# A row-variance kernel: sixteen-column loads in two buffers, a re-cut tail, the columns' last results stored apart, and the wait for the store moved behind the context's end

## The chip, the cores and the metric

The kernel runs on one core of one Trainium2 chip. The metric is the device time in microseconds of one execution. The kernel before takes 165.64 us (median of three runs, 165.6 to 165.7).

## What is computed

For each of 32 x 512 = 16,384 rows of 1,024 float32 values, the mean of the squares less the square of the mean, which is the row's variance:

```python
def setup_inputs():
    batch, seq, dim = 32, 512, 1024
    return {"x": np.random.randn(batch, seq, dim).astype(np.float32)}

def reference(x):
    mean_sq = np.mean(x**2, axis=-1)
    sq_mean = np.mean(x, axis=-1)**2
    return (mean_sq - sq_mean).astype(np.float32)
```

The input is 67.1 MB, the output 64 KB.

## The kernel before

The 16,384 rows are laid over 128 partitions, 128 rows to each partition. One row per partition, 128 rows in all, is called a *column*: a tile of 128 x 1024 float32, 512 KB. There are 128 columns. They form two blocks of memory (`BLOCKS`): the first 16 columns, and the other 112; within a block a partition's rows lie next to each other, so a load of n columns reads one run of n x 4 KB for each partition.

All loads are issued by SP, in order, through `load` (line 82), into one queue. The first 96 columns go in 12 loads of 8 (`GROUP`) into three buffers `xt` in turn (`NBUF`). A buffer is filled again only when `done` says that its former group is finished (line 127). The last 32 columns are the tail: loads of 8, 6, 6, 4, 3, 2 and 1 columns (`END_LOADS`), then the last two columns in two halves each. The first of these goes to `xt[0]`, the others to `xt_end`, which nothing else uses, so SP issues all of them in a row after a single wait (line 129).

Two engines work on each group. DVE (VectorE) computes a column's statistics with two `bn_stats` of 512 elements (line 100) and joins them with one `bn_aggr` (line 163), which gives mean and variance. ACT (ScalarE) needs two passes over a column: a copy scaled by -S/D that sums up to the negative mean (line 104), and a square with that mean as bias that sums up to the variance (line 109). In each group of 8, ACT has the first three columns (`NACT`), DVE the other five. DVE takes the group's arrival (`landed`), lets ACT go, and its last `bn_aggr` waits for ACT's `act_done` before it signals `done`. Both engines run this part as a loop of four turns (`Fori`) of three groups. GpSimd copies the variances of a turn from `stage` to `mv` (line 146).

In the tail, `END_WHO` gives one letter for each column: A for ACT, D for DVE. DVE's order there: first half of a column, the aggregate of the column before, second half (lines 175 to 183). The last two columns are D, each of their halves with a wait of its own (lines 186 to 199). ACT takes its columns load by load: all means, then all variances (lines 217 to 232).

SP, after the loads, stores the results of the first block (16 columns, once `copied` is up), waits for the last steps of ACT and DVE, and stores the other 112 columns. Then it clears the semaphores and waits for both stores to land (lines 235 to 242). All of this stands in one critical section (line 123). When it has ended, the tile context closes (its code has line 268 in the profile): every engine drains, they meet, and GpSimd clears the context's semaphores.

`head_slot` places the head of each loop at instruction 128 of a block of the instruction stream.

Of the kernel before, what the change touches and what calls it, by code (L numbers as in the profile page):

```python
# [7 lines left out]


# [1 line left out]
def kernel(  # L11
# [10 lines left out]

    nc = tc.nc
    P = nc.NUM_PARTITIONS
    FP32 = mybir.dt.float32
    ACTF = mybir.ActivationFunctionType
    ENG = mybir.EngineType

    xf = x.flatten_outer_dims()
    N, D = xf.shape
    assert N % P == 0
    ncols = N // P
    H = D // 2
    S = D ** -0.5

    SMALL = 16
    BLOCKS = [(0, SMALL, 0), (SMALL, ncols - SMALL, SMALL * P)]

    GROUP = 8
    NBUF = 3
    TURNS = 4
    PER_TURN = NBUF * GROUP
    END0 = TURNS * PER_TURN
    NACT = 3
    END_LOADS = [8, 6, 6, 4, 3, 2, 1]
    END_WHO = "AAADDDDD" "AADDDD" "AADDDD" "DADD" "DAD" "AD" "A"
    IN_HALVES = 2
    HEAD = 128  # L50

    pool = ctx.enter_context(tc.tile_pool(name="pool", bufs=1))
    xt = [pool.tile([P, GROUP, D], FP32, name=f"xt{b}") for b in range(NBUF)]
    xt_end = pool.tile([P, ncols - END0 - GROUP, D], FP32, name="xt_end")
    mv = pool.tile([P, 2, ncols], FP32, name="mv")
    stage = pool.tile([P, PER_TURN, 2], FP32, name="stage")
    stats = pool.tile([P, PER_TURN, 2, 6], FP32, name="stats")
    stats_end = pool.tile([P, ncols - END0, 2, 6], FP32, name="stats_end")
    neg_mean = pool.tile([P, PER_TURN], FP32, name="neg_mean")
    neg_mean_end = pool.tile([P, ncols - END0], FP32, name="neg_mean_end")  # L60
    psum = ctx.enter_context(tc.tile_pool(name="psum", bufs=1, space=bass.MemoryType.PSUM))
    junk = [pool.tile([P, D], mybir.dt.bfloat16, name=f"junk{i}") for i in range(NACT)]
    junk_sq = [psum.tile([P, D], FP32, name=f"junk_sq{i}") for i in range(NACT)]

    sync, act, dve, gps = nc.sync, nc.scalar, nc.vector, nc.gpsimd
    landed = [nc.alloc_semaphore(f"landed{b}") for b in range(NBUF)]
    NEND = len(END_LOADS) + 2 * IN_HALVES
    landed_end = [nc.alloc_semaphore(f"landed_end{b}") for b in range(NEND)]
    go = nc.alloc_semaphore("go")
    act_done = nc.alloc_semaphore("act_done")  # L70
    done = nc.alloc_semaphore("done")
    copied = nc.alloc_semaphore("copied")
    dve_step = nc.alloc_semaphore("dve_step")
    act_step = nc.alloc_semaphore("act_step")
    stored = nc.alloc_semaphore("stored")
    sems = [*landed, *landed_end, go, act_done, done, copied, dve_step, act_step]

    def load(dst, c0, n, sem, f0=0, f=D):
        b0, pitch, row0 = next(b for b in BLOCKS if b[0] <= c0 < b[0] + b[1])
# [4 lines left out]
            in_=dataclasses.replace(xf, offset=(row0 + c0 - b0) * D + f0, ap=ap),  # L84
        ).then_inc(sem, 16)

    def store(block):
        b0, pitch, row0 = block
        sync.dma_start(
            out=dataclasses.replace(out, offset=row0, ap=[[pitch, P], [1, pitch]]),  # L90
            in_=mv[:, 1, b0 : b0 + pitch],
        ).then_inc(stored, 16)

    def take(engine, sem, n):
        engine.wait_ge(sem, n)
        engine.sem_inc(sem, -n)  # L96
# [6 lines left out]
    def act_mean(i, xcol, nm):  # L103
        return act.activation(  # L104
            out=junk[i], in_=xcol, func=ACTF.Copy, scale=-S / D, accum_out=nm
        )

    def act_var(i, xcol, nm, var):
        return act.activation(  # L109
            out=junk_sq[i], in_=xcol, func=ACTF.Square, scale=S, bias=nm, accum_out=var  # L110
        )

    end_cols = []
    at = END0
    for b, n in enumerate(END_LOADS):
        for k in range(n):
            c = at + k
            col = xt[0][:, k, :] if b == 0 else xt_end[:, c - END0 - GROUP, :]
            end_cols.append((b, c, col))
        at += n  # L120
    assert at == ncols - IN_HALVES

    with tc.tile_critical(no_gpsimd_drain=True):  # L123

        for g in range(TURNS * NBUF):
            if g >= NBUF:
                sync.wait_ge(done, g - NBUF + 1)
            load(xt[g % NBUF], g * GROUP, GROUP, landed[g % NBUF])
        sync.wait_ge(done, TURNS * NBUF - NBUF + 1)
        load(xt[0], END0, GROUP, landed_end[0])  # L130
        c = END0 + GROUP
        for b, n in enumerate(END_LOADS[1:], 1):
            k = c - END0 - GROUP
            load(xt_end[:, k : k + n, :] if n > 1 else xt_end[:, k, :], c, n, landed_end[b])
            c += n
        b = len(END_LOADS)
        for c in range(c, ncols):
            for h in range(2):
                dst = xt_end[:, c - END0 - GROUP, h * H : (h + 1) * H]
                load(dst, c, 1, landed_end[b], h * H, H)  # L140
                b += 1

        gps.sem_inc(copied, 1)
        for t in range(TURNS):
# [2 lines left out]
                out=mv[:, 1, t * PER_TURN : (t + 1) * PER_TURN], in_=stage[:, :, 1]  # L147
            ).then_inc(copied, 1)

        with nc.Fori(0, TURNS, engines=[ENG.DVE], head_slot={ENG.DVE: HEAD}):  # L150
            take(dve, copied, 1)
            for b in range(NBUF):
                take(dve, landed[b], 16)
                dve.sem_inc(go, 1)
                mine = range(b * GROUP + NACT, (b + 1) * GROUP)
                for j in mine:
                    last = halves(stats[:, j, :, :], xt[b][:, j - b * GROUP, :])
                last.then_inc(dve_step, 1)
                take(dve, dve_step, 1)
                for j in mine:  # L160
                    if j == mine[-1]:
                        take(dve, act_done, 1)
                    last = dve.bn_aggr(out=stage[:, j, :], in_=stats[:, j, :, :])  # L163
                last.then_inc(done, 1)
        n = 0
        waiting = None
        seen = -1
        for b, c, col in end_cols:
            if END_WHO[c - END0] != "D":
                continue  # L170
            if b != seen:
                dve.wait_ge(landed_end[b], 16)
                seen = b
            st = stats_end[:, c - END0, :, :]
            dve.bn_stats(out=st[:, 0, :], in_=col[:, :H])  # L175
            if waiting:
                waiting()
            n += 1
            dve.bn_stats(out=st[:, 1, :], in_=col[:, H:]).then_inc(dve_step, 1)  # L179

            def waiting(n=n, c=c, st=st):
                dve.wait_ge(dve_step, n)
                dve.bn_aggr(out=mv[:, :, c], in_=st)  # L183

        b = len(END_LOADS)
        for c in range(ncols - IN_HALVES, ncols):
            st = stats_end[:, c - END0, :, :]
            col = xt_end[:, c - END0 - GROUP, :]
            dve.wait_ge(landed_end[b], 16)
            dve.bn_stats(out=st[:, 0, :], in_=col[:, :H])  # L190
            waiting()
            dve.wait_ge(landed_end[b + 1], 16)
            n += 1
            dve.bn_stats(out=st[:, 1, :], in_=col[:, H:]).then_inc(dve_step, 1)  # L194
            b += 2

            def waiting(n=n, c=c, st=st):
                dve.wait_ge(dve_step, n)
                return dve.bn_aggr(out=mv[:, :, c], in_=st)  # L199

        waiting().then_inc(dve_step, 1)
        dve_steps = n + 1

        act.preload_act_table(ACTF.Square)  # L204
        with nc.Fori(0, TURNS, engines=[ENG.Activation], head_slot={ENG.Activation: HEAD}):
            for b in range(NBUF):
                take(act, go, 1)
                mine = range(b * GROUP, b * GROUP + NACT)
                for i, j in enumerate(mine):
                    last = act_mean(i, xt[b][:, i, :], neg_mean[:, j : j + 1])  # L210
                last.then_inc(act_step, 1)
                take(act, act_step, 1)
                for i, j in enumerate(mine):
                    last = act_var(i, xt[b][:, i, :], neg_mean[:, j : j + 1], stage[:, j, 1:2])
                last.then_inc(act_done, 1)
        n = 0
        for b in range(len(END_LOADS)):
            mine = [(c, col) for bb, c, col in end_cols if bb == b and END_WHO[c - END0] == "A"]
            if not mine:
                continue  # L220
            act.wait_ge(landed_end[b], 16)
            for i, (c, col) in enumerate(mine):
                k = c - END0
                last = act_mean(i, col, neg_mean_end[:, k : k + 1])
            n += 1
            last.then_inc(act_step, 1)
            act.wait_ge(act_step, n)
            for i, (c, col) in enumerate(mine):
                k = c - END0
                last = act_var(i, col, neg_mean_end[:, k : k + 1], mv[:, 1, c : c + 1])  # L230
            n += 1
            last.then_inc(act_step, 1)
        act_steps = n

        sync.wait_ge(copied, 1)
        store(BLOCKS[0])
        sync.wait_ge(act_step, act_steps)
        sync.wait_ge(dve_step, dve_steps)
        store(BLOCKS[1])
        sync.sem_clear(range(sems[0].num, sems[-1].num + 1))  # L240
        sync.wait_ge(stored, 32)
        sync.sem_clear(stored)


# [28 lines left out]
```

## Time and profile before

| | us |
|---|---|
| median of three runs | 165.64 |
| the profiled execution | 165.63 |
| its span, first to last instruction | 163.7 |
| DVE busy | 107.0 (65%) |
| ACT busy | 107.3 (66%) |
| GpSimd busy | 1.0 (1%) |
| moved by DMA | 67.19 MB, mean 411 GB/s |
| one `bn_stats` of 512 elements in the loop | 0.679 (they overlap: ten take 6.03) |
| one aggregate in the loop | 0.177 (they overlap: four take 0.42) |
| ACT's mean, variance of a column | 1.045, 1.104 |

How to read it: the span runs from the first to the last instruction; the time of an execution also holds what lies around it. DVE's and ACT's durations are those of single instructions, and neighbouring ones overlap, so that sums are made from the starts of rows. In the row of slices each digit is the busy share of a fortieth of the span, in tenths. The chain of waits is followed back from the last instruction: at each step to what released it. A name with a q (SPq, DVEq) is an engine's sequencer, which waits for semaphores and issues DMAs.

### The profile page before, as it was taken

What the parts mean: (1) busy time and instruction counts of PE and PEld (TensorE: products, weight loads), DVE (VectorE), ACT (ScalarE), POOL (GpSimd) and SP (SyncE); (2) the same over time, 40 slices, a digit from 0 to 9 for tenths busy, and PEclk for the clock granted to TensorE, in tenths of its full rate; (3) what the DMA queues carried; (4) which work ended last, traced back from release to release, by engine and by line L of the source; (5) the groups of instructions that cost most, each with busy time, mean ns of one, the idle gap of its engine ahead of it and who ended that gap; (6) DMA issues with size and microseconds to landing.
All of it is one profiled execution on the core that took longest, in us unless ns stands there. A gap on an engine that the chain in (4) does not pass through costs nothing. (4 is left out here: it accounts for less than half of the span.)

```text
span 163.7 us, 615 instructions
## 1 busy us (share of the span) xinstructions
DVE 107.0 (65%) x243; ACT 107.3 (66%) x189; POOL 1.0 (1%) x8
## 2 busy tenths in 40 slices
DVE  0005929487492957839296692948749397859993
ACT  3005939488493957939397593948849398759692
POOL 0000000000000000000000000000000000000000
DMA  6999999999998999999999989999999999999980
GB/s 204 432 400 480 400 424 472 392 488 400 408 488 384 440 456 392 480 408 400 480 400 424 472 384 464 432 400 480 400 408 488 406 396 468 396 430 412 405 297 14
DMA packets 3602, 67.19 MB, mean 411 GB/s; under 512 B 656, under 2 KB 656, under 8 KB 1296
## 3 DMA queue, kind: packets, MB, share of 16 engines
q1 hardware_dynamic: 3600, 67.18, 96.2%
q14 instruction: 2, 0.02, 0.0%
HBM read 67.11 MB, written 0.07 MB: 410 GB/s over the span
## 5 line engine op out<-in xcount | busy, mean ns | idle before, releaser
L100 DVE BATCH_NORM_STATS2 stats<-xt 128x6 f32<-128x512 f32 x120 | 72.4, 679 | 41.1 <-DVEq L96 41.1
L104 ACT ACTIVATE junk<-xt 128x1024 bf16<-128x1024 f32 x39 | 40.7, 1045 | 45.9 <-ACTq L96 43.3
L109 ACT ACTIVATE junk_sq<-xt,neg_mean 128x1024 f32<-128x1024 f32 x36 | 39.7, 1104 | 1.5
L163 DVE BATCH_NORM_AGGREGATE stage<-stats 128x2 f32<-128x12 f32 x60 | 7.6, 177 | 6.9 <-DVEq L96 5.2
L104 ACT ACTIVATE junk<-xt_end 128x1024 bf16<-128x1024 f32 x8 | 8.4, 1050 | 4.9 <-DMA xt_end<-in_x_dram 4.8
L175 DVE BATCH_NORM_STATS2 stats_end<-xt_end 128x6 f32<-128x512 f32 x14 | 9.5, 679 | 3.2 <-DMA xt_end<-in_x_dram 3.2
L109 ACT ACTIVATE junk_sq<-xt_end,neg_mean_end 128x1024 f32<-128x1024 f32 x8 | 8.9, 1113 | 0.2
L179 DVE BATCH_NORM_STATS2 stats_end<-xt_end 128x6 f32<-128x512 f32 x14 | 9.0, 640 | 0.0
L104 ACT ACTIVATION_READ_ACCUMULATOR junk<-xt 128x1 f32 x39 | 7.2, 186 | 0.0
L109 ACT ACTIVATION_READ_ACCUMULATOR junk_sq<-xt,neg_mean 128x1 f32 x36 | 6.7, 186 | 0.0
L175 DVE BATCH_NORM_STATS2 stats_end<-xt 128x6 f32<-128x512 f32 x5 | 3.4, 681 | 2.3 <-DMA xt<-in_x_dram 2.3
L183 DVE BATCH_NORM_AGGREGATE mv<-stats_end 128x2 f32<-128x12 f32 x19 | 3.7, 194 | 0.0
L109 ACT ACTIVATE junk_sq<-xt,neg_mean_end 128x1024 f32<-128x1024 f32 x3 | 3.3, 1104 | 0.0
L179 DVE BATCH_NORM_STATS2 stats_end<-xt 128x6 f32<-128x512 f32 x5 | 3.2, 648 | 0.0
L204 ACT ACT_TABLE_LOAD x1 | 1.3, 1283 | 0.9 <-SPq L123 0.9
L190 DVE BATCH_NORM_STATS2 stats_end<-xt_end 128x6 f32<-128x512 f32 x2 | 1.4, 695 | 0.4 <-DMA xt_end<-in_x_dram 0.4
L146 POOL COPY mv<-stage 128x24 f32<-128x24 f32 x4 | 0.8, 204 | 127.0 <-DVE stage L163 127.0
L109 ACT ACTIVATION_READ_ACCUMULATOR junk_sq<-xt_end,neg_mean_end 128x1 f32 x8 | 1.5, 186 | 0.0
L104 ACT ACTIVATION_READ_ACCUMULATOR junk<-xt_end 128x1 f32 x8 | 1.5, 186 | 0.0
L194 DVE BATCH_NORM_STATS2 stats_end<-xt_end 128x6 f32<-128x512 f32 x2 | 1.3, 650 | 0.0
L109 ACT ACTIVATION_READ_ACCUMULATOR junk_sq<-xt,neg_mean_end 128x1 f32 x3 | 0.6, 186 | 0.0
L199 DVE BATCH_NORM_AGGREGATE mv<-stats_end 128x2 f32<-128x12 f32 x2 | 0.4, 202 | 0.0
(4 smaller groups left out, 0.4 us busy)
## 6 DMA issues: line engine op xcount, KB each, us to landing
xt<-in_x_dram SPq DMA_DIRECT2D x13, 4096.0 KB, 21.6
xt_end<-in_x_dram SPq DMA_DIRECT2D x2, 3072.0 KB, 32.0
xt_end<-in_x_dram SPq DMA_DIRECT2D x1, 2048.0 KB, 39.8
xt_end<-in_x_dram SPq DMA_DIRECT2D x1, 1536.0 KB, 43.1
xt_end<-in_x_dram SPq DMA_DIRECT2D x1, 1024.0 KB, 45.1
xt_end<-in_x_dram SPq DMA_DIRECT2D x4, 256.0 KB, 42.0
xt_end<-in_x_dram SPq DMA_DIRECT2D x1, 512.0 KB, 45.9
out_dram<-mv SPq DMA_DIRECT2D x1, 56.0 KB, 1.6
```

What stands on the lines that cost most here:

```text
L100: last = dve.bn_stats(out=st[:, h, :], in_=xcol[:, h * H : (h + 1) * H])
L104: return act.activation(out=junk[i], in_=xcol, func=ACTF.Copy, scale=-S / D, accum_out=nm)
L109: return act.activation(out=junk_sq[i], in_=xcol, func=ACTF.Square, scale=S, bias=nm, accum_out=var)
L146: gps.tensor_copy(out=mv[:, 1, t * PER_TURN : (t + 1) * PER_TURN], in_=stage[:, :, 1]).then_inc(copied, 1)
L163: last = dve.bn_aggr(out=stage[:, j, :], in_=stats[:, j, :, :])
L175: dve.bn_stats(out=st[:, 0, :], in_=col[:, :H])
L179: dve.bn_stats(out=st[:, 1, :], in_=col[:, H:]).then_inc(dve_step, 1)
L183: dve.bn_aggr(out=mv[:, :, c], in_=st)
L190: dve.bn_stats(out=st[:, 0, :], in_=col[:, :H])
L194: dve.bn_stats(out=st[:, 1, :], in_=col[:, H:]).then_inc(dve_step, 1)
L199: return dve.bn_aggr(out=mv[:, :, c], in_=st)
L204: act.preload_act_table(ACTF.Square)
```

## The change

The loop now has three turns of two groups, with 16 columns in each load: six loads fill two buffers in turn. In each group ACT has six columns, in two batches of three means and three variances, and DVE ten. The tail's loads are 8, 8, 5, 4, 2, 2, 1 and 1 columns and the two halves of the last one; the first two go to the halves of `xt[0]`, the others to `xt_end`, now of 16 columns.

DVE no longer aggregates its eleven columns of the tail's first two loads. It leaves their statistics in `stats_join`, and GpSimd joins them in eleven steps, each behind a semaphore of the step before, and writes `mv`.

There are three stores: columns 0 to 15; columns 16 to 120, after GpSimd's last step, ACT's fourth load and DVE's first column of the fifth; and the last 7 columns at the end. The context's semaphores are now allocated with the context, which clears them at its end, and the critical section is led by GpSimd rather than SP. The wait for the three stores stands behind the context's end. The alignment to instruction 128 of a block is asked for once on ACT and DVE, ahead of the section, and no longer at the loops.

```diff
-    GROUP = 8
-    NBUF = 3
-    TURNS = 4
+    GROUP = 16
+    NBUF = 2
+    TURNS = 3
...
-    NACT = 3
-    END_LOADS = [8, 6, 6, 4, 3, 2, 1]
-    END_WHO = "AAADDDDD" "AADDDD" "AADDDD" "DADD" "DAD" "AD" "A"
-    IN_HALVES = 2
+    NACT = 6
+    ACT_BATCH = 3
+    END_LOADS = [8, 8, 5, 4, 2, 2, 1, 1]
+    END_WHO = "AADDDDDD" "AAADDDDD" "AADDD" "AADD" "DD" "AD" "D" "A"
+    FIRST = END_LOADS[0] + END_LOADS[1]
+    JOINED = END_WHO[:FIRST].count("D")
+    PIECES = [512, 512]
+    EARLY = 4
...
-    landed = [nc.alloc_semaphore(f"landed{b}") for b in range(NBUF)]
+    landed = [tc.alloc_semaphore(f"landed{b}") for b in range(NBUF)]
...
+    for engine in (act, dve):
+        engine.addr_align(FETCH_BLOCK_INSTRUCTIONS, offset=HEAD, max_nops=0)
+
+    with tc.tile_critical(sync_engine=ENG.Pool, no_gpsimd_drain=True):
...
+        gps.wait_ge(dve_step, 1)
+        steps = [
+            lambda: gps.tensor_tensor(out=two, in0=mean[:, :, 0:2], in1=mean[:, :, 2:4], op=ALU.add),
...
+        for k, step in enumerate(steps):
+            if k:
+                gps.wait_ge(gps_step, k)
+            step().then_inc(gps_step, 1)
...
-        with nc.Fori(0, TURNS, engines=[ENG.DVE], head_slot={ENG.DVE: HEAD}):
+        with nc.Fori(0, TURNS, engines=[ENG.DVE]):
...
+            if c in joined:
+                last = halves(stats_join[:, joined.index(c), :, :], col)
+                if c == joined[-1]:
+                    last.then_inc(dve_step, 1)
+                    n += 1
+                continue
...
         sync.wait_ge(copied, 1)
-        store(BLOCKS[0])
+        store(0, SMALL)
+        sync.wait_ge(gps_step, gps_steps)
+        sync.wait_ge(act_step, act_step_of[EARLY - 1])
+        sync.wait_ge(dve_step, dve_step_of[EARLY])
+        store(SMALL, early)
         sync.wait_ge(act_step, act_steps)
         sync.wait_ge(dve_step, dve_steps)
-        store(BLOCKS[1])
-        sync.sem_clear(range(sems[0].num, sems[-1].num + 1))
-        sync.wait_ge(stored, 32)
-        sync.sem_clear(stored)
+        store(early, ncols)
+
+    ctx.close()
+    tc.close()
+    tc.compile()
+    sync.wait_ge(stored, 48)
+    sync.sem_clear(stored)
```

## The prediction

> **What bounds the kernel now.** I read the page's 40 slices first, then the chain that ended last, then the loads one by one (start of issue plus time to landing), then the last three microseconds.
>
> ```profile
> DMA  6999999999998999999999989999999999999980
> GB/s 204 432 400 480 400 424 472 392 488 400 408 488 384 440 456 392 480 408 400 480 400 424 472 384 464 432 400 480 400 408 488 406 396 468 396 430 412 405 297 14
> q1 hardware_dynamic: 3600, 67.18, 96.2%
> DMA 28%; DVE 2%; SPq 2%; issue 0%
> ```
>
> The DMA engines are full from the second slice to the last but one, while DVE and ACT are busy for 65% and 66%. The input stream is the bound, and the compute engines have slack everywhere but at the end. The groups of 8 columns start on DVE at 13.94 and, eleven later, at 120.80: 9.715 us each, 1.214 us a column, 432 GB/s.
>
> ```profile
> 111.85 46.08 DMA xt_end<-in_x_dram
> ...
> 157.96 0.69 DVE stats_end L190
> 158.65 0.11 DVE mv L183
> 158.76 0.57 DVE stats_end L194
> 159.33 0.64 DVE stats_end L190
> 159.98 0.11 DVE mv L199
> 160.08 0.57 DVE stats_end L194
> 160.65 0.02 issue
> 160.67 0.21 DVE mv L199
> ```
>
> The chain's tail (start, duration): the first half of column 126 lands at 157.93, then four halves and their aggregates run without idle time to 160.88.
>
> ```profile
> xt_end<-in_x_dram SPq DMA_DIRECT2D x1, 256.0 KB, 30.8
> 129.08 6.35 SPq L82 DMA_DIRECT2D xt_end<-in_x_dram  x1
> 160.98 0.34 SPq L89 DMA_DIRECT2D out_dram<-mv  x1
> out_dram<-mv SPq DMA_DIRECT2D x1, 56.0 KB, 1.6
> L242 SPq EVENT_SEMAPHORE_RANGE_CLEAR  x1: 25/25/25, 162.6 to 162.6; - x1
> L268 POOLq EVENT_SEMAPHORE  x4: 17/17/17, 163.1 to 163.6; - x4
> ```
>
> The very last half is issued at 129.08 and lands at 129.08+30.8 = 159.88, just before DVE takes it at 160.00. So the data chain and the DVE chain end together; from last landing to the end of the last aggregate is 1.00 us. Then the store: issued 160.98, landed 162.58. Only then (the clear at 162.6) does the context's end begin, a run of drains and semaphore exchanges up to 163.6; the span ends at 163.7. That is 1.1 us of end after the landing. The profiled execution took 165.63, so 1.93 us lie around its span; the median of the runs is 165.64, the same.
>
> **The change part by part.**
>
> *Loads.* Twelve loads of 8 columns become six of 16, and eleven tail loads become ten: 23 become 16. What does a load cost beyond its bytes? From 120.80 to 159.88 the last 32 columns took 39.08 us in 11 loads; at the steady pace 4 loads take 38.86. Seven more loads cost 0.22, 0.03 each. Measured from 130.33 instead (108.63+21.7, the landing of the tail's first 8): 24 columns in 10 loads took 29.55 against 29.15 in three, 0.06 each. I take 0.045 x 7 = 0.3 us earlier for the last landing: 159.58. No load with runs of 64 KB is in the trace; runs of 32, 24 and 16 KB take 1.214, 1.217 and 1.217 us a column, so it should matter little. Bounds: 0 if a long run behaves as two short ones, 0.7 at 0.1 a load (single columns, 157.28-156.0 = 1.28 against 1.214, show 0.07).
>
> One page limits this from above: the Trainium skill, "DMA: Bandwidth & Descriptors", section "Where 436 GB/s comes from", puts the ceiling of a core's ports at 435.2 GB/s. The steady 432 is 0.8% below it, so by the page the 96 columns could gain 0.9 us at most; the sum by that would be 163.8. No run here shows whether the ceiling is reached.
>
> *Two buffers in place of three.* A load into a buffer waits for its `done`. Now: the group that landed at 120.80 has its last aggregate at 127.83+0.21 = 128.04, 7.24 us, limited by ACT (three columns, 120.84 to 127.69, 6.85). With 16 columns: ACT 2 x 6.85 = 13.7, DVE 20 x 0.603 + 10 x 0.106 = 13.1, so `done` comes 14.1 us after landing. SP issues in 0.43, and first packets move some 0.6 after an issue begins (0.94 to about 1.5 at the start): new data at about 15.2. The other buffer holds 16 x 1.214 = 19.4 us of stream; packets run about 1.1 us ahead of the landing (at the end they fade at 158.75, the landing is 159.88), so the queue would run dry at 18.3. Cover 3.1 us, cost nothing. If it were gone, each microsecond too late costs one on each of five refills. The longer first load delays DVE's first work by 9.7 us, beside the stream, at no cost.
>
> *Tail on DVE and ACT.* I keep the columns' landing times of before and number them by columns landed: 104 at 130.3, 112 at 140.0, 117 at 146.1, 121 at 151.0, 123 at 153.5, 125 at 156.0, 126 at 157.3, 127 at 158.58, then halves at 159.23 and 159.88. DVE at 1.26 us a column (1.21 without the aggregate in the first 16) is done before each next landing or within 0.1 us of it: 137.6, 146.0, 149.9, 153.5, 156.05, 157.3, 158.55. From the first half's landing it needs 0.02+0.69+0.11+0.57+0.02+0.21 = 1.62, to 160.85, as before. ACT: a batch of two takes 4.59 (137.62 to 142.21): 146.9 after the batch of three, 151.4, 156.0, one column to 158.4, then the column landing at 158.58, which takes 2.41 (158.32 to 160.73): 161.0. So ACT, not DVE, ends last, by 0.15. With the 0.3 taken off: ACT 160.71, DVE 160.55, store issued 0.10 later at 160.81 (before 160.98).
>
> *GpSimd's eleven steps.* They replace eleven aggregates and follow DVE's last joined column (146.0). Nearest row: the copy of 128x24, 204 ns, released 0.06 after DVE's end: 11 x 0.26 = 2.9 us; bounds 1.1 (memsets at 0.10) and 5.8 (twice, for two inputs and 44 elements). All of it lies in the 10 us until ACT finishes the fourth load at 156.0, for which the same store waits.
>
> *Stores.* SP now waits for GpSimd, ACT and DVE, then issues columns 16 to 120 at about 156.1; behind that wait stands only the last store, 4.7 us later. The early store's packets queue behind the last loads and need about 0.2 us of the engines (the 56 KB store: 29% of 0.5 us and 23% of 0.3 us), gone by 159.5. The ring is still full at the start of the tail (the second half waits 8.46 us to issue now); that blocks SP to about 148, when nothing else is due. The last store has 28-byte runs. Price: 1.6 by the 56 KB row, 1.4 if its 0.2 of transfer vanishes; 1.8 if the transfer part doubles. I take 1.6: landed 162.41.
>
> Against small stores stands the Trainium skill, "DMA: Bandwidth & Descriptors", "Rules for kernel authors": transfers under 64 KB pay mostly overhead and should be joined. The row agrees that 1.4 of 1.6 us are overhead, which is why splitting saves so little; by that page's fixed 2 us (its section on the anatomy of one DMA, given there for GpSimd's path) the sum would be 164.8.
>
> *The wait behind the end.* SP's last wait moves behind the drains and clears. They start when the store is issued and, at 1.12 us (162.58 to 163.7), end near 160.81+0.34+1.12 = 162.27, under the store's flight. No row shows the new order: I allow 0.1 (a second range clear, 69 ns in this trace) to 0.56 (half its length again, for more exchanges). Left after the landing: the wait and a 25 ns clear, about 0.09. Span 162.5, plus 1.93: **164.4 us**. The parts: end hidden -1.0, loads -0.3, ACT's tail +0.13.
>
> *Start.* SP is released by GpSimd rather than releasing itself: all engines pass the start within 0.1 us (ACT's table load 0.91, SP's first load 0.94). 0, at most 0.1.
>
> **The rivals.** *The end is not hidden.* If the new end waits for something that itself comes after the store, or is longer by more than 0.56, the gain shrinks to the stream's: 164.85 to 165.6. For: the order of the end changes and its rows are only shown for the old order. Against: none of the drains moves data, and they were all idle for 1.1 us of waiting. Chance 0.14, of which 0.04 within the band of no change.
>
> *Large loads pay more.* At 0.1 us a load, with the store at 1.4: 164.4-0.4-0.2 = 163.8, down to 163.3 with a smoother start (the first 8 columns land at 13.74, 3.1 us more than 8 x 1.214 after the first issue begins). Chance 0.14.
>
> *The stream runs dry* (the slower side). If landing to refill takes over 18.3 us rather than 15.2, the engines idle at each of the five refills. Decisive point: the gain of 1.2 and the band's 0.3 are eaten at 0.3 us each, that is at 18.6 us; at 19.3 us it costs 5 us and gives 169.4. For: only one load is queued while one is worked on, where two were. Against: the 3.1 us of cover; both engines' groups repeat here to 0.1 us. Chance 0.09.
>
> **How the numbers follow.** The sum's case, 163.95 to 164.85, has 0.63; its time is the prediction. A measurement tells from no change what is over 0.2%, 0.33 us. Faster: 0.63+0.14+0.10 = 0.87; same 0.04; slower 0.09. The range 163.5 to 165.2 takes in the price of the last store, the loads' 0 to 0.7 and most of the unhidden end; it leaves out the dry stream and the fringes, some 0.17.
>
> **What would show it.** Right: groups of 16 start 19.3 to 19.45 us apart; the DMA row stays at 9; the last landing is near 159.6; the last store issue follows an ACT row of the last single column by 0.1; the drains stand before the store's landing and the span ends within 0.2 us of it. Wrong: zeros or sevens in the DMA row every 19 us (dry stream), DVE or ACT idle inside a group, GpSimd's last step after 156, or drains after the store's landing.

## The result and the profile after

The changed kernel takes 163.65 us (median of four runs, 163.54 to 163.67), against 165.62 for the kernel before on the same chip. The ratio is 0.9879, with a 95% interval of 0.9865 to 0.9892. That is 1.97 us less, where 1.24 had been forecast; the time lies near the lower end of the stated range. The profiled execution took 163.64 with a span of 161.9.

First the page of the changed kernel: the slices of the DMA engines and the load queue.

```profile
DMA  7969979989988998998997997997989999999991
q1 hardware_dynamic: 2736, 67.18, 96.7%
```

The stream is still the bound. The packets fell from 3600 to 2736. A load of 128 partitions makes 128 packets and 16 completions, a store the same: 16 loads and 3 stores give 19 x 144 = 2736, so a run of 64 KB is one packet. The prediction had named sevens in the slices as a sign of a dry stream. Here they are not idle time: the load queue is busy for 96.7% of the span, and from the first data (1.89) to the last landing (158.94) there are only 97.0% of it. A packet of 64 KB takes 2.42 us of a slice's 4.05, and the page puts it down whole to the slice in which it starts. The groups' starts show the pace. In the timeline of DVE, start and duration of the first two groups of 16 (ahead of the brackets, what was run; in them, the idle time before):

```profile
23.11 11.96 DVE L113 BATCH_NORM_STATS2 stats<-xt 128x6 f32<-128x512 f32 x20 [23.11 <-DVEq L109]
...
36.89 0.21 DVE L216 BATCH_NORM_AGGREGATE stage<-stats 128x2 f32<-128x12 f32 x1 [0.89 <-DVEq L109]
42.44 11.96 DVE L113 BATCH_NORM_STATS2 stats<-xt 128x6 f32<-128x512 f32 x20 [5.33 <-DVEq L109]
```

The same place in the kernel before, its second group of 8, which also completes the first 16 columns:

```profile
23.65 6.03 DVE L100 BATCH_NORM_STATS2 stats<-xt 128x6 f32<-128x512 f32 x10 [2.47 <-DVEq L96]
```

So 0.54 us are won before the first 16 columns have landed. Then a group of 16 takes 19.33 (42.44-23.11), 19.35 in the mean of five, where two groups of 8 took 19.43; the sixth starts at 119.84 where 120.80 stood, 0.96 earlier, of which the five groups gave 0.42. DVE sits idle 5.3 us before a group because it waits for data, and the pace shows that no refill came too late.

The chain that ended last, after:

```profile
117.84 39.74 DMA xt_end<-in_x_dram
157.58 0.02 issue
157.61 1.16 ACT junk L117 x2
158.76 0.02 issue
158.79 1.12 ACT junk_sq L122
159.91 0.12 ACTq L144
```

It runs through ACT's last single column, landed at 157.58, to 160.03. The issues of the last half and of the last store, with their times to landing:

```profile
xt_end<-in_x_dram SPq DMA_DIRECT2D x1, 256.0 KB, 40.1
...
out_dram<-mv SPq DMA_DIRECT2D x1, 3.5 KB, 1.4
```

```profile
118.84 7.59 SPq L93 DMA_DIRECT2D xt_end<-in_x_dram  x1
...
160.06 0.33 SPq L100 DMA_DIRECT2D out_dram<-mv  x1
```

The last half lands at 118.84+40.1 = 158.94 (before 159.88), the last store is issued 1.12 later (before 1.10) and lands at 161.46. The context's end, by line (duration shortest, median, longest in ns, first and last start):

```profile
L308 DVEq DRAIN  x2: 19/65/111, 160.0 to 161.5; - x2
L308 POOLq EVENT_SEMAPHORE_RANGE_CLEAR  x2: 64/101/138, 161.1 to 161.4; - x2
L308 POOLq EVENT_SEMAPHORE  x4: 17/17/17, 160.9 to 161.7; - x4
```

It now starts under the store's flight, and ends after the landing, at 161.87; SP's final clear is at 161.9. From the last store's issue to the span's end 1.84 pass (161.9-160.06), where 2.72 did. So of the 1.99 us between the two profiled executions, 0.94 come from the stream, of which 0.02 are lost again before the last store's issue, 0.88 from the end, and 0.19 from what lies around the span (163.64-161.9 = 1.74, before 1.93).

### The profile page after: what moved, and what is told of

Its sections match the earlier page's. It is cut to its first block, busy times and chain, and to the rows that moved or that the text cites. A ratio compares the mean times of both kernels' runs of the same rounds, so it can differ in the third digit from the quotient of the medians.

```text
span 161.9 us, 579 instructions
## 1 busy us (share of the span) xinstructions
DVE 103.7 (64%) x232; ACT 106.3 (66%) x189; POOL 3.6 (2%) x18
## 3 DMA queue, kind: packets, MB, share of 16 engines
q1 hardware_dynamic: 2736, 67.18, 96.7%
## 5 line engine op out<-in xcount | busy, mean ns | idle before, releaser
L117 ACT ACTIVATE junk<-xt 128x1024 bf16<-128x1024 f32 x41 | 42.7, 1042 | 50.4 <-ACTq L109 49.3
L113 DVE BATCH_NORM_STATS2 stats_join<-xt 128x6 f32<-128x512 f32 x22 | 13.2, 677 | 0.0
L216 DVE BATCH_NORM_AGGREGATE stage<-stats 128x2 f32<-128x12 f32 x60 | 6.0, 166 | 6.2 <-DVEq L109 5.3
L122 ACT ACTIVATE junk_sq<-xt_end,neg_mean_end 128x1024 f32<-128x1024 f32 x6 | 6.7, 1111 | 0.1
L117 ACT ACTIVATE junk<-xt_end 128x1024 bf16<-128x1024 f32 x6 | 6.3, 1046 | 0.4 <-DMA xt_end<-in_x_dram 0.2
L235 DVE BATCH_NORM_STATS2 stats_end<-xt_end 128x6 f32<-128x512 f32 x9 | 6.1, 675 | 0.0
L239 DVE BATCH_NORM_STATS2 stats_end<-xt_end 128x6 f32<-128x512 f32 x9 | 5.8, 642 | 0.0
L122 ACT ACTIVATE junk_sq<-xt,neg_mean_end 128x1024 f32<-128x1024 f32 x5 | 5.5, 1106 | 0.1
L165 POOL COPY mv<-stage 128x32 f32<-128x32 f32 x3 | 0.6, 210 | 133.0 <-DVE stage L216 133.0
L244 DVE BATCH_NORM_AGGREGATE mv<-stats_end 128x2 f32<-128x12 f32 x9 | 1.7, 191 | 0.0
L251 DVE BATCH_NORM_STATS2 stats_end<-xt_end 128x6 f32<-128x512 f32 x2 | 1.3, 668 | 0.1
## 6 DMA issues: line engine op xcount, KB each, us to landing
xt_end<-in_x_dram SPq DMA_DIRECT2D x1, 2048.0 KB, 34.2
```

The costliest lines, as they stand in the source:

```text
L113: last = dve.bn_stats(out=st[:, h, :], in_=xcol[:, h * H : (h + 1) * H])
L117: return act.activation(out=junk[i], in_=xcol, func=ACTF.Copy, scale=-S / D, accum_out=nm)
L122: return act.activation(out=junk_sq[i], in_=xcol, func=ACTF.Square, scale=S, bias=nm, accum_out=var)
L165: gps.tensor_copy(out=mv[:, 1, t * PER_TURN : (t + 1) * PER_TURN], in_=stage[:, :, 1]).then_inc(copied, 1)
L251: last = dve.bn_stats(out=st[:, i, :], in_=end_col(c)[:, f : f + size])
```

## The experiments

Each run was timed in five rounds beside the kernel before, whose median on those chips was 165.63 to 165.75. The intervals of the ratios are about 0.3% wide, so differences of 0.1 or 0.2 us are read from the traces.

**Where the stream gained.** Two loads for each group of 16:

```diff
-            load(xt[g % NBUF], g * GROUP, GROUP, landed[g % NBUF])
+            for h in range(0, GROUP, 8):
+                load(xt[g % NBUF][:, h : h + 8, :], g * GROUP + h, 8, landed[g % NBUF])
...
-                take(dve, landed[b], 16)
+                take(dve, landed[b], 32)
```

> Each of the six 16-column loads is issued as two of 8 columns; buffers, waits and the tail stay. Theory (the stream gained by fewer and longer loads): groups start 19.43 us apart as before instead of 19.33, the first group on DVE at about 23.6 instead of 23.11, in all 0.5 + 0.5: about 164.65. Rival (the stream gained by something else, two deep buffers or fewer waits on SP): spacing stays 19.33, first group stays at 23.11, 163.65.

163.92 us, ratio 0.9888 (0.9873 to 0.9903).

```profile
23.12 11.96 DVE L113 BATCH_NORM_STATS2 stats<-xt 128x6 f32<-128x512 f32 x20 [23.12 <-DVEq L109]
42.55 11.96 DVE L113 BATCH_NORM_STATS2 stats<-xt 128x6 f32<-128x512 f32 x20 [5.44 <-DVEq L109]
```

The pace is back at 19.43, so 0.08 us a group (19.43 less 19.35) belongs to the loads. The first group stays at 23.12: the 0.5 at the start does not. That half of my theory fell. The first load alone in two parts:

```diff
+            if g == 0:
+                load(xt[0][:, 0:8, :], 0, 8, first_half)
+                load(xt[0][:, 8:16, :], 8, 8, landed[0])
+                continue
...
+        dve.wait_ge(first_half, 16)
         with nc.Fori(0, TURNS, engines=[ENG.DVE]):
```

> Only the very first load is issued as two of 8 columns. Theory A (a long first load starts the stream better): the first group on DVE at 23.5 to 23.65 instead of 23.11, spacing stays 19.33, about 164.1. Theory B (every load costs the same 0.1 us, the start among them): the first group at 23.2, 163.75.

163.57 us, ratio 0.9872 (0.9857 to 0.9887), first group at 22.95, pace 19.35. A long first load gives nothing at the start; theory B's 0.1 does not show there either.

Are the 0.08 a price of the load or of the packet? One load with two separate runs for each partition:

```diff
+            c0 = SMALL + 8 * (g - 1)
+            sync.dma_start(
+                out=xt[g % NBUF].rearrange("p (r k) d -> p r (k d)", r=2),
+                in_=dataclasses.replace(
+                    xf, offset=(row0 + c0 - b0) * D,
+                    ap=[[pitch * D, P], [40 * D, 2], [1, 8 * D]],
+                ),
+            ).then_inc(landed[g % NBUF], 16)
```

> The loads of groups 1 to 5 stay single loads of 16 columns, but each partition reads two separate runs of 32 KB instead of one of 64 KB (256 packets a load, one completion); the results of columns 16 to 95 stand in other rows than in the reference. If the length of a run decides: spacing 19.43, about 164.15. If the number of loads (its completion) decides: spacing 19.33, 163.65.

163.97 us, ratio 0.9894 (0.9879 to 0.991).

```profile
22.95 11.96 DVE L113 BATCH_NORM_STATS2 stats<-xt 128x6 f32<-128x512 f32 x20 [22.95 <-DVEq L109]
42.36 11.97 DVE L113 BATCH_NORM_STATS2 stats<-xt 128x6 f32<-128x512 f32 x20 [5.42 <-DVEq L109]
```

One load, one completion, and yet 19.41, and 19.42 in the mean of five, the pace of the short runs. The length of the run decides: 128 packets fewer are worth 0.08 us. Shared out over 16 engines these are eight each, at some 10 ns.

**The start.** What else differs there? The page of both kernels has two packets of a queue named "instruction". In the kernel before, the queue's line in the window from 2 to 3 us (packets, MB, share of 16 engines):

```profile
q14 instruction: 1, 0.01, 4.3%
```

The other one falls between 3 and 4. After the change, from 1 to 2 us, about when the first data move:

```profile
q14 instruction: 2, 0.02, 8.5%
```

The alignment put back to the heads of the loops:

```diff
-    for engine in (act, dve):
-        engine.addr_align(FETCH_BLOCK_INSTRUCTIONS, offset=HEAD, max_nops=0)
...
-        with nc.Fori(0, TURNS, engines=[ENG.DVE]):
+        with nc.Fori(0, TURNS, engines=[ENG.DVE], head_slot={ENG.DVE: HEAD}):
```

(and the same for ACT).

> The alignment stands at the heads of the two loops again and not ahead of the section. Theory A (fetching of instructions at the start disturbs the first loads, and the early alignment moves it): the first group on DVE at 23.6 instead of 23.1, 164.1. Theory B (the start differs for another reason): 23.1, 163.65.

164.33 us, ratio 0.9916 (0.9902 to 0.993). Its instruction queue from 4 to 6 us, and its first group:

```profile
q14 instruction: 2, 0.02, 1.9%
```

```profile
23.59 11.97 DVE L113 BATCH_NORM_STATS2 stats<-xt 128x6 f32<-128x512 f32 x20 [23.59 <-DVEq L109]
```

The 0.5 is lost again and stays lost: the last store is issued at 160.56 instead of 160.06. And what lies around the span is 1.93 again (164.23-162.3), as in the kernel before, and 1.89 to 1.95 over all its executions; in those of the eleven other runs told of here, all with the early alignment, it is 1.70 to 1.84. The other way round, this edit alone in the kernel before:

> The kernel before, with one edit: the alignment to slot 128 stands ahead of the section on ACT and DVE instead of at the heads of their loops. Theory (the 0.5 at the start belongs to the two packets of instructions alone, which then move before the first load's data): both packets of instructions before 2.0, the second group on DVE at 23.1 instead of 23.65, every later landing 0.5 earlier, 165.1. Rival (it needs the long loads too): 165.64.

165.22 us, ratio 0.997 (0.9959 to 0.9981). Both packets lie between 1 and 2 us, and DVE's second group starts here:

```profile
22.90 6.03 DVE L101 BATCH_NORM_STATS2 stats<-xt 128x6 f32<-128x512 f32 x10 [2.46 <-DVEq L97]
```

The second group is 0.75 earlier and the last store's issue 0.73 (160.25, before 160.98). The gain is the alignment's place, not the long loads'. The time fell by only 0.48, as the end grew (below).

How do two packets do this? The trace also keeps the start and the duration of each DMA packet, and a packet that starts as another ends is the next one on the same engine, so that the 16 engines can be followed one by one. In the kernel before, the engine with the instruction packet of 3.91 ends its share of the first 16 columns last, at 22.96, and the next one at 22.45. With the alignment back at the loops' heads, the two engines with the packets of 5.08 and 5.11 are last, at 22.78 and 22.89, and the next one ends at 22.60. In the changed kernel the packets start at 1.77 and 1.92, and neither of their engines is last; the last one ends at 22.54. A load has landed when the last of its 16 engines is done, and a fetch behind the first data puts one engine behind the others. A few tenths remain open: over the runs with the early alignment the first 16 columns are taken anywhere from 22.90 to 23.44.

**The end.** The wait put back into the section:

```diff
         store(early, ncols)
+        sync.wait_ge(stored, 48)
+        sync.sem_clear(stored)
...
-    sync.wait_ge(stored, 48)
-    sync.sem_clear(stored)
```

> The wait for the three stores is put back into the critical section. Theory (the end's exchanges take some 1.45 us from SP's arrival and now run under the store's flight of 1.4): they start at the landing again, span end about 160.06+1.4+0.05+1.45 = 162.95, about 164.7. The prediction's own sizes (1.1 us of end after the landing) give 162.6, 164.4. Rival (moving the wait gains nothing): 163.65.

164.56 us, ratio 0.9931 (0.9917 to 0.9944), span 162.8. SP waits again before the end can start:

```profile
SPq L306 <- DMA out_dram<-mv: 1.1, 1, 1.1
```

From the last store's issue (159.98) to the span's end 2.82 pass instead of 1.84: moving the wait is worth 1.0 in the span, 0.9 in the time. After the landing at 161.38 the end takes 1.42, where the kernel before needed 1.1. Three runs looked for these 0.3. SP in the lead, as before:

```diff
-    with tc.tile_critical(sync_engine=ENG.Pool, no_gpsimd_drain=True):
+    with tc.tile_critical(no_gpsimd_drain=True):
```

> The critical section is led by SP again instead of GpSimd, at its start and its end; all else stays. Theory (the span now ends with the exchanges of the end, 1.8 us after the last store's issue, and GpSimd's lead makes them longer: 1.42 us after the landing in the run with the wait inside, 1.1 in the kernel before): the end takes 1.1 from SP's arrival at 160.4, so the store's landing at 161.46 comes last, span about 161.55, 163.3. If the earlier start of the stream (first 16 columns taken at 23.1 instead of 23.65) is due to the lead, 0.5 is lost again at the start, 163.8. Rival (the lead is nothing): 163.65.

163.77 us, ratio 0.988 (0.9865 to 0.9896); from the store to the end 160.32 to 162.2, 1.88. The lead is nothing; my theory fell. One range to clear instead of two:

```diff
-    landed = [tc.alloc_semaphore(f"landed{b}") for b in range(NBUF)]
+    landed = [nc.alloc_semaphore(f"landed{b}") for b in range(NBUF)]
...
         store(early, ncols)
+        sync.sem_clear(range(sems[0].num, sems[-1].num + 1))
```

(and so for the other semaphores).

> The section's semaphores are allocated apart from the context and cleared by SP right after the last store's issue, as before the change, so that the context's end has one range to clear instead of two; the wait for the stores stays behind the end. Theory (the second clear and its drain make the end 0.3 longer, and the end now comes after the landing): from the last store's issue to the span's end 1.5 instead of 1.82, the landing nearly last, 163.35. Rival (another part of the end is longer): 1.8, 163.65.

163.67 us, ratio 0.9881 (0.9866 to 0.9897); span 162.0, its last store issued at 160.2, 1.8 before the end. The second clear is not the reason by itself. The end of this run:

```profile
L310 DVEq DRAIN  x2: 19/65/111, 160.1 to 161.6; - x2
L310 POOLq EVENT_SEMAPHORE_RANGE_CLEAR  x1: 69/69/69, 161.2 to 161.2; - x1
```

GpSimd is done earlier now, but DVE's last drain, of 111 ns, stands at 161.6. The kernel before with only the early alignment has one clear and SP in the lead, and its end after the landing is 1.45 long (161.85 to 163.3). There too DVE's drain is late:

```profile
L272 DVEq DRAIN  x2: 10/60/111, 162.0 to 163.0; - x2
```

In the kernel before DVE's two drains take 10 ns each, the last at 163.3 beside the other engines'. So two things seem to lie side by side, a second clear on GpSimd and a late drain on DVE, and taking one away uncovers the other. The other half of this is on record too: with the alignment at the loops' heads, and in the two runs at slots 144 and 96 told of below, there are two clears, but DVE's last drain takes 10 ns beside the other engines', and from the last store's issue to the span's end it is still 1.73 to 1.75 (160.56 to 162.3, 161.35 to 163.1, 161.37 to 163.1). The late drain thus comes and goes with the place of DVE's instructions and costs some 0.1 beside a second clear. Why it is late is not shown, and a run without both was not made.

One store of columns 16 to 127 at the end:

```diff
-        sync.wait_ge(act_step, act_step_of[EARLY - 1])
-        sync.wait_ge(dve_step, dve_step_of[EARLY])
-        store(SMALL, early)
         sync.wait_ge(act_step, act_steps)
         sync.wait_ge(dve_step, dve_steps)
-        store(early, ncols)
+        store(SMALL, ncols)
```

> Columns 16 to 127 leave in one store at the end, 56 KB, as before the change; the early store is gone. Theory (the end's exchanges finish 1.8 us after the last issue, so a landing 1.6 after it is covered too): 163.65. Rival (the landing ends the span): 0.2 more, 163.85.

163.63 us, ratio 0.9877 (0.9862 to 0.9892), span 161.9. Splitting the store gains nothing: what ends last is the context's end, not the landing.

**The GpSimd join.** DVE aggregates its eleven columns itself:

```diff
-            if c in joined:
+            if False:
...
-        sync.wait_ge(gps_step, gps_steps)
```

> DVE aggregates its eleven columns of the tail's first two loads itself, as the others; GpSimd's eleven steps and the wait for them are gone. Theory (the tail begins on DVE only at 133.8, when the last group of 16 is done, and DVE is late from there on): 11 x 0.106 more on DVE ends 1.1 later, less 0.14 for ACT's lead: about +1.0, 164.6. Prediction's view (DVE waits for data at each load of the tail): 163.65.

164.40 us, ratio 0.992 (0.9907 to 0.9934). The time is near the theory's, but the trace shows another reason. From its timeline:

```profile
156.11 1.06 ACT L117 ACTIVATE junk<-xt_end 128x1024 bf16<-128x1024 f32 x1 [1.22 <-DMA xt_end<-in_x_dram]
...
159.28 0.69 DVE L217 BATCH_NORM_STATS2 stats_end<-xt_end 128x6 f32<-128x512 f32 x1 [0.21 <-DMA xt_end<-in_x_dram]
```

Both engines wait for data. The load that ACT waits for here lands 1.07 later than in the changed kernel (116.94+39.1 = 156.04 against 116.87+38.1 = 154.97); up to the load before it all landings agree to 0.2. In between, from 153.0 to 153.5 us, the trace has a third packet of instructions:

```profile
q14 instruction: 1, 0.01, 4.1%
```

DVE's instructions had filled the 128 slots behind the alignment almost to the last: the trace shows 71 for the loop and 53 for the tail. Eleven aggregates more cross into the next block of 256. Two runs separate the causes. First the same work as in the changed kernel, with DVE's instructions 16 slots further on:

```diff
-        engine.addr_align(FETCH_BLOCK_INSTRUCTIONS, offset=HEAD, max_nops=0)
+        engine.addr_align(
+            FETCH_BLOCK_INSTRUCTIONS, offset=HEAD + 16 if engine is dve else HEAD, max_nops=0
+        )
```

> DVE's instructions are placed 16 slots further on in their block of 256 (144 instead of 128), so that the tail's last ones cross into the next block; no operation differs. Theory (fetching a block while the loads stream holds back one DMA engine and with it every later landing; this, not DVE's work, made the run without the GpSimd join late): a third packet of instructions in the trace, in the tail, the last landings about 1.0 later, 164.6. Rival (the late landings there came from DVE's extra work): 163.65.

164.60 us, ratio 0.993 (0.9917 to 0.9944). The packet is there, from 149 to 150 us, and DVE waits for the last column:

```profile
q14 instruction: 1, 0.01, 2.1%
```

```profile
159.55 0.69 DVE L253 BATCH_NORM_STATS2 stats_end<-xt_end 128x6 f32<-128x512 f32 x1 [0.51 <-DMA xt_end<-in_x_dram]
```

No operation differs, and the time is 0.95 longer. In the profiled execution (164.86) one of the first two packets also fell behind 2 us, and the first group starts 0.33 late, at 23.44 (the run with SP in the lead, with both packets ahead of 2 us, has 23.36, so this may be scatter); the tail's fourth load and all behind it then land another 1.0 later (35.2 after its issue, 34.2 in the changed kernel). The fetch alone delays the landings.

Followed engine by engine, the trace shows the size of it. The instruction packet starts at 149.31 and takes 0.33, and the data packet of 16 KB behind it on its engine takes 1.27, where the others take 0.62. That engine is then 0.98 behind, and every later landing waits for it. In the run without the join it is 0.33, and then 0.97 where 8 KB take 0.31: again 0.98.

Second, DVE's own aggregates again, with more room in the block:

```diff
-    HEAD = 128
+    HEAD = 96
```

> DVE aggregates its eleven columns itself, as in the run without the join, but its and ACT's instructions begin at slot 96, so that DVE's still fit into the block. Theory: two packets of instructions, landings as in the changed kernel (last column's first half at 158.2); DVE reaches it 0.87 late, at 159.1 (its start in the run without the join less its 0.21 of waiting), ends at 160.7, last store issued at 160.8, +0.7: 164.35. Rival (DVE's work alone makes the landings late): last landing at 160 again, store issued at 161.1.

164.61 us, ratio 0.9934 (0.992 to 0.9947). No packet in the tail, but none at the start either. One came between 36 and 40 us, amid the second group's load, and one between 46 and 52, amid the third's:

```profile
q14 instruction: 1, 0.01, 0.3%
```

The groups' starts, and DVE's last row:

```profile
22.99 11.96 DVE L113 BATCH_NORM_STATS2 stats<-xt 128x6 f32<-128x512 f32 x20 [22.99 <-DVEq L109]
43.22 11.97 DVE L113 BATCH_NORM_STATS2 stats<-xt 128x6 f32<-128x512 f32 x20 [6.24 <-DVEq L109]
...
161.08 0.21 DVE L224 BATCH_NORM_AGGREGATE mv<-stats_end 128x2 f32<-128x12 f32 x1
```

The second group comes 20.23 after the first, 0.9 more than elsewhere; later groups are 19.36 apart again, and the 0.9 stays. So the first packet cost 0.9 and the second nothing. Followed engine by engine, the first lost 0.89 (0.31, and 3.00 for 64 KB in place of 2.42). The second packet fell on another engine, which lost 0.62 (0.31, and 2.73) and so it was still ahead of the first. Here DVE runs through the tail without a wait and ends at 161.29, 1.40 after the changed kernel's 159.89. The stream is only 0.9 late; the other half microsecond is DVE's own. So both causes are real: the join keeps DVE inside its block, and it takes work from an engine with no slack.

## Why the prediction was right, and where it was not

*Direction and range* were right, and the likeliest case was passed by 0.75 us on the good side. The time lies where the rival *Large loads pay more* had put it (163.8 down to 163.3, chance 0.14), but that is in part luck: a load did cost nearly its 0.1 and the store 1.4, while its smoother start came from the alignment, the store's landing no longer counts, and 0.19 lie outside the span.

*Two buffers.* Forecast: `done` 14.1 us after a group's landing and no dry stream. Measured 14.0 (23.11 to 37.10). Right, and so was the case against the dry stream. One reading under it was off: the kernel before moves its first data at 1.98, 1.04 after the issue began, not 0.6; since I had added the issue's 0.43 besides, the 15.2 stands.

*Loads.* The term of 0.3 us was mis-sized. The long loads gave 0.42 over five groups, 0.08 for each 128 packets saved, nearly twice the 0.045 that I took from the mixed tail; and it belongs to the packets, not, as I wrote, to the load.

*Start.* This step failed: "0, at most 0.1". I looked at when the engines are released, and not at when the two packets of instructions move, though the page names their queue and the diff moves the alignment. It was the largest part of what I missed: 0.5 us in the stream, and more around the span.

*Tail on DVE and ACT.* The sum held, its working did not. I let DVE begin the tail's first load at its landing, 130.3. The last group of 16 keeps it until 133.8:

```profile
133.62 0.21 DVE L216 BATCH_NORM_AGGREGATE stage<-stats 128x2 f32<-128x12 f32 x1 [0.88 <-DVEq L109]
133.81 11.37 DVE L113 BATCH_NORM_STATS2 stats_join<-xt 128x6 f32<-128x512 f32 x19
```

From there DVE never waits until 158.28, where it arrives 0.08 before the data. What I costed as idle was used up, and GpSimd's join, which I priced as hidden work of no effect, is what makes DVE arrive in time. ACT does end last, by 0.14 (forecast 0.15).

*GpSimd's steps.* Forecast 2.9 us of work; measured from 147.04 to 150.64, 3.6, well within the cover.

*Stores.* The early store is free, as forecast, and useless: the single store gave the same time. The last one took 1.4, the lower bound.

*The end.* Forecast 1.0 hidden; 0.9 in the span. The end's exchanges take 1.47 (160.40 to 161.87), 0.35 more than the old ones and within what I allowed, and so they, not the landing, end the span. The sign that I had named for it failed: the last drains (161.5) stand just behind the landing (161.46), and the span ends 0.4 after it, not within 0.2.

*Around the span.* I kept 1.93; it is 1.74, and it went back to 1.93 with the alignment at the loops' heads. So 0.19 hangs on the alignment too, which is then worth 0.68 of the 1.97 us (164.33-163.65). With the wait (164.56-163.65 = 0.91) and the long loads (0.27 and 0.32 in the two runs that put short ones back) that makes 1.86 to 1.91, nearly the whole. What happens outside the span is in no view.

## What to carry to other kernels

In a kernel bound by its loads, see where the instruction queue's packets fall in the trace: before the first data they cost little here, behind it up to 1.07 us, more than all the longer runs gained. Count the instructions of a loop and its tail against the block before adding any, and take the longest contiguous runs that the buffers hold. When a wait is moved under something else, check which of the two ends last; here a cheaper store gained nothing, because the end had become the longer one.

## What the runs showed of the hardware

A packet of instructions takes some 0.3 us of one engine's time (4.1% of 16 engines in 0.5 us), but three of the four that were fetched in mid-stream put every later landing back by 0.9 to 1.07 us; the fourth, in the run at slot 96, cost nothing, as another engine was already later. Two of them just after the start cost 0.5 to 0.75. The loss is larger than the packet because the data packet behind it on the same engine takes longer too, by 0.58 to 0.66 in the three cases that counted. Why it does is not shown. The Trainium skill, "Runtime: NRT & Kernel Launch", section "Instruction fetch mechanics", says that an engine fetches blocks of 256 instructions over a queue of its own and that crossing a block is mostly hidden. The separate queue agrees with these traces, and DVE's instructions, once they ran past the 128 slots behind slot 128, brought one more packet; the size of a block is not seen, each packet being 0.01 MB. Hidden it was not: the load stream keeps the engines busy for 96.7% of the span.

Longer packets brought the steady rate from 431.8 to 433.5 GB/s (8.389 MB in 19.43 and in 19.35 us). The ceiling of 435.2 that the prediction took from the Trainium skill ("DMA: Bandwidth & Descriptors", "Where 436 GB/s comes from") was not passed, and what is left under it is 0.4%.
